# Transposes in groups inside two matrix products, and a reordered attention softmax, in a two-block transformer kernel

## Chip, cores and metric

One core of one Trainium2 chip. The metric is the device time of one execution in microseconds (us); a kernel's time is the median of its runs.

## Reference

Two transformer blocks on one sequence of 256 tokens, width 2048, float32. The change touches two steps of the first block, the attention over a memory of 256 tokens and the feed-forward step behind it:

```python
def memory_cross_attention(hn, mn, wq, wk, wv, wo):
    q = (hn @ wq).reshape(b, s, XA_HEADS, XA_HEAD_DIM)      # 4 heads of 128
    ...
    scores = jnp.einsum('bshd,bmhd->bhsm', q, k) * (XA_HEAD_DIM ** -0.5)
    probs = jax.nn.softmax(scores, axis=-1)
    o = jnp.einsum('bhsm,bmhd->bshd', probs, v).reshape(b, s, XA_WIDTH)
    return o @ wo

h = h + memory_cross_attention(rmsnorm(h, xa_norm_w), rmsnorm(mem, mem_norm_w), wq, wk, wv, wo)
u = rmsnorm(h, ffn_norm_w)
h = h + jnp.square(jax.nn.relu(u @ w1)) @ w2                 # w1: 2048 x 8192
```

Ahead of these stand the mixers and the product with `w_out`, behind them the second block with its experts.

## The kernel before

The products with weights are split into three: a weight is cast to a rounded half `wh` (ACT, line 289) and a remainder `wl` (DVE, line 290), the activation likewise into `uh` and `ul`, and PE sums `wh*uh + wh*ul + wl*uh`. Weights arrive in pieces of 1 MB (`raw`, three buffers), each holding four of the 16 chunks of 128 rows; `wsplit` casts two chunks at a time into `wh` and `wl`, of which there are three buffers each, so six chunks are cast at most ahead of PE. A cast of chunks 12 and 13 takes the buffer of chunks 6 and 7 and waits until PE has done with these. `gemm_T` takes 12 products of 256 columns per chunk, 192 in all, into one PSUM accumulator `acc` (two buffers).

The activation has to be transposed for it. `to_T` does this by chunks: two transposes on PE (line 254) into a PSUM tile `mx`, then ACT writes `uh` (line 367) and DVE writes `ul` (line 368), which needs `uh`. In `xattn` and in `ffn` all 16 chunks are asked for ahead of the product, then `rstd` takes the row norms: eight squares with sums on ACT (line 340) and a chain of some thirteen tiny operations on DVE (lines 355 to 273). The softmax needs them as its scale, lines 982 and 984; the feed-forward step needs them only when `w2`'s products are added.

In `xattn` the queries of all four heads are copied out of PSUM by one ACT instruction (line 987). Then, for each pair of heads, PE takes four score products, DVE the maximum (line 1000) and its scaled negative (line 1001), ACT the exponentials with their sums (line 1004), DVE the reciprocal and the scaling (lines 1006 and 1008), PE transposes the probabilities, DVE copies them (line 1017), and PE multiplies by the values.

All along DVE also works on something else: products of a modulation matrix for the second block (`macc`, line 830), fed by 512 KB loads.

The order on each engine isn't that of the source: a scheduler in the compiler sets it, and each engine then takes its own queue strictly in that order, stopping at an instruction whose input isn't there. The stretch in question is 773 to 873 us of the span.

Of the kernel before, what the change touches and what calls it, by code (L numbers as in the profile page):

```python
# [182 lines left out]
class Prog:  # L183
# [110 lines left out]

    def gemm_To(self, srcs, uh, ul, outs, widths):
        ncol = sum(widths)
        kg = srcs[0].shape[1]
        nk = kg * len(srcs)
        offs = [sum(widths[:j]) for j in range(len(widths))]
        for g, src in enumerate(srcs):  # L300
            for kc, h, l in self.wsplit(src, ncol):
                k = kg * g + kc
                for m, wd in enumerate(widths):
                    sl = slice(offs[m], offs[m] + wd)
                    for i, (a, b) in enumerate(((h, uh), (h, ul), (l, uh))):
                        self.mm(outs[m], a[:, sl], b[:, k, :], start=(k == 0 and i == 0 and m % 2 == 0),
                                stop=(k == nk - 1 and i == 2))

    def gemm_T(self, srcs, uh, ul):
        acc = self.acc()  # L310
        self.gemm_To(srcs, uh, ul, [acc[:, m * 256:m * 256 + 256] for m in range(4)], (128,) * 4)
        return acc
# [660 lines left out]
    def xattn(self):  # L973
        nc = self.nc
        r16 = lambda a: a.rearrange("p b (k t) -> p (b k) t", t=256)
        with ExitStack() as ctx:
            P = ctx.enter_context(self.tc.tile_pool(name="xa", bufs=2))
            uh, ul = r16(self.b16(F32R)), r16(self.b16(F32R))
            self.to_T([self.h[:, 0], self.h[:, 1]], lambda c: self.p("xa_w", c), uh, ul)
            rs = self.rstd(self.h)  # L980
# [3 lines left out]
            nc.vector.tensor_scalar(nsc, sc, -1.0, None, ALU.mult)  # L984
            acc = self.gemm_T([self.ins["wq"][g] for g in range(4)], uh, ul)
            qT = P.tile([128, 4, 256], F32, tag="qT", name="qT", bufs=1)
            nc.scalar.copy(qT, acc.rearrange("p (h t) -> p h t", h=4))
            xh = P.tile([128, 4, 256], F32R, tag="xh", name="xh", bufs=1)
            xl = P.tile([128, 4, 256], F32R, tag="xl", name="xl", bufs=1)
            S = lambda tag, n: self.smp.tile([128, n], F32, tag=tag, name=tag, bufs=2)  # L990
            for hp in range(2):
                ps = self.acc()
                for j in range(2):
                    h = hp * 2 + j
                    for tb in range(2):
                        o = j * 512 + tb * 256
                        self.mm(ps[:, o:o + 256], qT[:, h, tb * 128:tb * 128 + 128], self.kT[:, h], start=(tb == 0))
                mxv, nb, sm, ri = S("xmx", 4), S("xnb", 4), S("xsm", 4), S("xri", 4)
                v2 = lambda a: a.rearrange("p (j b) -> p j b", j=2)
# [26 lines left out]
    def ffn(self, extra):  # L1026
        nc = self.nc
        r16 = lambda a: a.rearrange("p b (k t) -> p (b k) t", t=256)
        with ExitStack() as ctx:
            P = ctx.enter_context(self.tc.tile_pool(name="ffn", bufs=2))  # L1030
            uh, ul = r16(self.b16(F32R)), r16(self.b16(F32R))
            self.to_T([self.h[:, 0], self.h[:, 1]], lambda c: self.p("ffn_w", c), uh, ul)
            rs = self.rstd(self.h)
            r2 = self.smp.tile([128, 2], F32, tag="r2", name="r2")
            nc.vector.tensor_tensor(r2, rs, rs, ALU.mult)

            def first(g):
                xh = P.tile([128, 8, 256], F32R, tag="fh", name="fh")
                xl = P.tile([128, 8, 256], F32R, tag="fl", name="fl")
                for j in range(2):  # L1040
                    acc = self.gemm_T([self.ins["w1"][g * 2 + j, k] for k in range(4)], uh, ul)
                    for b in range(2):
# [17 lines left out]
            self.final_init()  # L1060
            cur = first(0)
            for g in range(8):
                nxt = first(g + 1) if g < 7 else None
# [583 lines left out]
    def rows_hilo(self, P):  # L1647
# [4 lines left out]
        self.tc.keep_in_program_order(nc.vector.tensor_copy(rs2, self.rs))  # L1652
        self.busy(8)
        for q in range(4):
# [5 lines left out]

    def busy(self, n):
        ps = self.acc()
        for _ in range(n):
# [196 lines left out]
```

## Time and profile before

| | |
|---|---|
| median of 3 runs | 2301.49 us (2300.86, 2301.49, 2308.08) |
| the profiled execution | 2297.94 us, its span 2296.0 us |
| mean granted TensorE clock | 0.985 |
| PE busy (matmul) | 2165.3 us, 94% |
| DVE, ACT busy | 1502.9 us (65%), 892.8 us (39%) |
| DMA | 575.18 MB, mean 251 GB/s |

PE is TensorE's matmuls, PEld its weight loads, DVE VectorE, ACT ScalarE, SP the queue that issues the loads. Times are from the start of the span. "Idle before" an instruction is the time in which its engine stood, and `<-` names what released it.

### The profile page before, as it was taken

To read this page: it belongs to the slowest core of one execution; us is meant where nothing else is said; L and a number is where in the kernel's file an instruction comes from. 1 tells how busy PE (TensorE), PEld (TensorE's weight loads), DVE (VectorE), ACT (ScalarE), POOL (GpSimd) and SP (SyncE) were. 2 spreads that over 40 slices of the span, in tenths; PEclk is the share of its full clock that TensorE was granted. 3 is DMA by queue.
4 is the path that set the end of the run, shared out by engine and by line. 5 is a ranking of instruction groups with operands and counts; after the bars stand their busy time and mean duration, and the time that the engine had idled before them with its cause. 6 is when DMAs were issued, how large, how long until landed. Compare 5 with 4: busy or idle time off the path is not lost.

```text
span 2296.0 us, 40946 instructions
## 1 busy us (share of the span) xinstructions
PE 2165.3 (94%) x16688; PEld 1681.5 (73%) x16688; DVE 1502.9 (65%) x2561; ACT 892.8 (39%) x1445; POOL 61.4 (3%) x166
## 2 busy tenths in 40 slices
PE   6999999999999989999999999999999789888877
PEld 6888888888787779998998989988987442233222
DVE  6778887867768887778787787767657732222223
ACT  5444443444643444444444434446555211011000
POOL 1010000010100000000000000000000000000000
PEclk9999999999999999999999999999999999999899
DMA  7425443232278767887787787754445898999997
GB/s 255 146 96 184 157 165 134 95 114 93 86 284 310 282 251 260 289 304 268 263 313 257 258 314 259 268 183 156 167 164 195 332 379 367 393 395 421 420 421 319
DMA packets 101622, 575.18 MB, mean 251 GB/s; under 512 B 11548, under 2 KB 12700, under 8 KB 45880
## 3 DMA queue, kind: packets, MB, share of 16 engines
q1 hardware_dynamic: 101432, 572.55, 66.6%
q8 instruction: 132, 2.16, 0.4%
q14 instruction: 58, 0.48, 0.1%
HBM read 570.40 MB, written 2.10 MB: 249 GB/s over the span
## 4 chain that ended last, share of the span: by engine, by line
PE 75%; DMA 11%; DVE 9%; ACT 2%; issue 2%; SPq 0%; DVEq 0%; ACTq 0%
PE acc L250 43%; PE mx L250 30%; DMA mw<-wgu 4%; DMA mraw<-wmod 3%; DMA mw<-wd 2%; PE mx L254 2%; DVE wl L290 2%; DVE macc L830 1%; DMA row<-wmod 1%; DMA raw<-wd 1%; DMA b<-wgu 1%; ACT wh L289 0%; DMA raw<-wout 0%; DVE pr L1445 0%; DVE ey L1610 0%
## 5 line engine op out<-in xcount | busy, mean ns | idle before, releaser
L289 ACT CAST wh<-raw 128x1024 fp32r<-128x1024 f32 (+1 forms) x496 | 516.5, 1044 | 708.5 <-PE acc L250 521.9
L290 DVE TENSOR_TENSOR wl<-raw,wh 128x1024 fp32r<-128x1024 f32 (+1 forms) x496 | 599.0, 1213 | 191.6 <-ACT wh L289 189.2
L250 PE MATMUL acc<-b,wh 128*128 128x256 f32 x2560 | 467.4, 284 | 1.0 <-ACT b L367 1.0
L250 PE MATMUL mx<-b,wh 128*128 128x256 f32 (+1 forms) x2016 | 407.5, 292 | 0.7 <-ACT wh L289 0.7
L250 PEld LDWEIGHTS acc<-b,wh 128*128 128x128 f32 x2560 | 396.6, 189 | 3.2 <-ACT b L367 1.7
L250 PE MATMUL acc<-b,wl 128*128 128x256 f32 x1280 | 362.4, 283 | 0.6 <-DVE wl L290 0.6
L250 PEld LDWEIGHTS mx<-b,wh 128*128 128x128 f32 (+1 forms) x2016 | 314.9, 187 | 11.2 <-issue 3.3
L250 PE MATMUL mx<-b,wl 128*128 128x256 f32 (+1 forms) x1008 | 294.1, 292 | 0.8 <-DVE wl L290 0.8
L250 PEld LDWEIGHTS acc<-b,wl 128*128 128x128 f32 x1280 | 242.7, 190 | 1.7 <-DVE wl L290 1.4
L830 DVE SCALAR_TENSOR_TENSOR macc<-mraw,silc,macc 128x1024 f32<-128x1024 f32 x160 | 204.8, 1280 | 58.9 <-DMA mraw<-wmod 58.1
L250 PE MATMUL acc<-wh,fh 128*128 128x512 f32 x512 | 199.8, 390 | 0.0
L250 PE MATMUL acc<-wl,fh 128*128 128x512 f32 x512 | 199.3, 389 | 0.0
L250 PE MATMUL acc<-wh,fl 128*128 128x512 f32 x512 | 199.2, 389 | 0.0
L250 PEld LDWEIGHTS mx<-b,wl 128*128 128x128 f32 (+1 forms) x1008 | 188.2, 187 | 4.8 <-DVE wl L290 1.1
L250 PE MATMUL mx<-mw,xs 128*32 128x512 f32 (+1 forms) x512 | 122.8, 651 | 23.6 <-DMA mw<-wgu 21.7
L250 PE MATMUL acc<-wh,b 128*128 128x512 f32 x384 | 124.4, 402 | 1.0 <-ACT row L971 1.0
L250 PEld LDWEIGHTS acc<-wl,fh 128*128 128x128 f32 x512 | 96.1, 188 | 19.9
L250 PEld LDWEIGHTS acc<-wh,fl 128*128 128x128 f32 x512 | 96.1, 188 | 20.0
L250 PEld LDWEIGHTS acc<-wh,fh 128*128 128x128 f32 x512 | 96.1, 188 | 19.7
L250 PE MATMUL mx<-raw,xs 128*32 128x512 f32 (+1 forms) x328 | 98.1, 644 | 10.4 <-DMA raw<-wgu 10.4
L1580 DVE SCALAR_TENSOR_TENSOR eth<-eth,mx 128x256 f32<-128x256 f32 x9 | 3.8, 420 | 145.5 <-ACT eth L1579 145.5
L250 PEld LDWEIGHTS mx<-mw,xs 128*32 128x32 f32 (+1 forms) x512 | 26.8, 119 | 89.0 <-issue 44.2
(481 smaller groups left out, 2822.1 us busy)
## 6 DMA issues: line engine op xcount, KB each, us to landing
raw<-w SPq DMA_DIRECT2D x128, 1024.0 KB, 6.2
mraw<-wmod SPq DMA_DIRECT2D x160, 512.0 KB, 5.0
raw<-win SPq DMA_DIRECT2D x76, 1024.0 KB, 4.8
mw<-wgu SPq DMA_DIRECT2D x62, 1024.0 KB, 13.8
raw<-wgu SPq DMA_DIRECT2D x40, 1024.0 KB, 15.0
mw<-wd SPq DMA_DIRECT2D x28, 1024.0 KB, 15.1
raw<-wout SPq DMA_DIRECT2D x24, 1024.0 KB, 5.0
b<-wgu SPq DMA_DIRECT2D x23, 1024.0 KB, 10.9
```

The costliest lines, as they stand in the source:

```text
L250: return self.nc.tensor.matmul(out, lhsT=lhsT, rhs=rhs, start=start, stop=stop, skip_group_check=True)
L254: return self.nc.tensor.transpose(out, in_, self.ident[:k, :k])
L289: nc.scalar.copy(h[:, :n], rs)
L290: nc.vector.tensor_tensor(l[:, :n], rs, h[:, :n], ALU.subtract)
L830: nc.vector.scalar_tensor_tensor(a, b, self.silc[:, k:k + 1], a, ALU.mult, ALU.add)
L1580: nc.vector.scalar_tensor_tensor(th[:n], th[:n], 1.0, ps[:n, 0:256], ALU.add, ALU.mult)
```

## The change

The transposes are no longer asked for ahead of the product but inside it, four chunks before each weight piece, in `xattn` and in the first of `ffn`'s products. The norms (`rstd`) come after the product in the source, in `ffn` after the first two. The queries are copied out head by head, ACT and DVE in turn. The scores of all four heads are taken first, then seven products that nobody reads (`busy(7)`: a constant by a constant), then the softmax of both pairs.

```diff
@@ gemm_To
         for g, src in enumerate(srcs):
+            if before:
+                before(range(kg * g, kg * g + kg))
             for kc, h, l in self.wsplit(src, ncol):
...
@@ xattn
-            self.to_T([self.h[:, 0], self.h[:, 1]], lambda c: self.p("xa_w", c), uh, ul)
+            part = lambda ks: self.to_T([self.h[:, 0], self.h[:, 1]], lambda c: self.p("xa_w", c), uh, ul, ks)
+            acc = self.gemm_T([self.ins["wq"][g] for g in range(4)], uh, ul, part)
             rs = self.rstd(self.h)
...
-            acc = self.gemm_T([self.ins["wq"][g] for g in range(4)], uh, ul)
             qT = P.tile([128, 4, 256], F32, tag="qT", name="qT", bufs=1)
-            nc.scalar.copy(qT, acc.rearrange("p (h t) -> p h t", h=4))
+            for j in range(4):
+                (nc.vector.tensor_copy if j % 2 else nc.scalar.copy)(qT[:, j], acc[:, j * 256:j * 256 + 256])
...
+            scores = []
             for hp in range(2):
                 ps = self.acc()
...
                         self.mm(ps[:, o:o + 256], qT[:, h, tb * 128:tb * 128 + 128], self.kT[:, h], start=(tb == 0))
+                scores.append(ps)
+            self.busy(7, self.mx("lg"))
+            for hp, ps in enumerate(scores):
                 mxv, nb, sm, ri = S("xmx", 4), S("xnb", 4), S("xsm", 4), S("xri", 4)
@@ ffn
-            self.to_T([self.h[:, 0], self.h[:, 1]], lambda c: self.p("ffn_w", c), uh, ul)
-            rs = self.rstd(self.h)
-            r2 = self.smp.tile([128, 2], F32, tag="r2", name="r2")
-            nc.vector.tensor_tensor(r2, rs, rs, ALU.mult)
+            part = lambda ks: self.to_T([self.h[:, 0], self.h[:, 1]], lambda c: self.p("ffn_w", c), uh, ul, ks)
...
-                    acc = self.gemm_T([self.ins["w1"][g * 2 + j, k] for k in range(4)], uh, ul)
+                    acc = self.gemm_T([self.ins["w1"][g * 2 + j, k] for k in range(4)], uh, ul, None if g or j else part)
...
             cur = first(0)
+            rs = self.rstd(self.h)
+            r2 = self.smp.tile([128, 2], F32, tag="r2", name="r2")
+            nc.vector.tensor_tensor(r2, rs, rs, ALU.mult)
@@ busy
-    def busy(self, n):
-        ps = self.acc()
+    def busy(self, n, ps):
         for _ in range(n):
             self.tc.keep_in_program_order(self.mm(ps[:, 0:256], self.ones, self.c("run")))
```

What the scheduler makes of it is seen in three places. Lines of the changed kernel stand three to eight higher than those of before (370 for 367, 371 for 368, 343 for 340, 833 for 830, 1008 for 1000, 1012 for 1004). First, ACT from the second weight piece of `wq` to the exponentials; `wh<-raw` are casts of weights, `b_10231` is `uh`, `mx,ss` the squares, `qT` the queries. Before:

```order
L367 ACTIVATE b_10231<-mx,prm 128x256 x2
L289 CAST wh<-raw 128x1024
L367 ACTIVATE b_10231<-mx,prm 128x256 x11
L340 ACTIVATE mx,ss<-h 128x512
L367 ACTIVATE b_10231<-mx,prm 128x256
L340 ACTIVATE mx,ss<-h 128x512 x7
L289 CAST wh<-raw 128x1024 x7
L987 COPY qT<-acc 128x1024
L1004 ACTIVATE pr,xsm<-acc,xnb,xsc 128x256 x8
```

and in the changed kernel:

```order
L289 CAST wh<-raw 128x1024 x3
L370 ACTIVATE b_10231<-mx,prm 128x256 x4
L289 CAST wh<-raw 128x1024 x2
L370 ACTIVATE b_10231<-mx,prm 128x256 x3
L343 ACTIVATE mx,ss<-h 128x512
L370 ACTIVATE b_10231<-mx,prm 128x256
L343 ACTIVATE mx,ss<-h 128x512 x7
L289 CAST wh<-raw 128x1024
L991 COPY qT<-acc 128x256
L289 CAST wh<-raw 128x1024
L991 COPY qT<-acc 128x256
L1012 ACTIVATE pr,xsm<-acc,xnb,xsc 128x256 x8
```

The evacuations of chunks 8 to 15 and the eight squares, ahead of the last seven casts before, now stand among them, four chunks behind a cast each time, and the squares only two casts ahead of the exponentials.

Second, DVE from the last casts ahead of the scores to the first scaling of probabilities; `rs_`, `xsc` and `xnsc` are the chain of the norms, `xmx` the maxima, `xnb` what the exponentials wait for. Before:

```order
L290 TENSOR_TENSOR wl<-raw,wh 128x1024
L830 SCALAR_TENSOR_TENSOR macc<-mraw,silc,macc 128x1024
L290 TENSOR_TENSOR wl<-raw,wh 128x1024
L830 SCALAR_TENSOR_TENSOR macc<-mraw,silc,macc 128x1024
L1000 TENSOR_REDUCE xmx<-acc 128x4
L1001 TENSOR_TENSOR xnb<-xmx,xnsc 128x4
L1000 TENSOR_REDUCE xmx<-acc 128x4
L1001 TENSOR_TENSOR xnb<-xmx,xnsc 128x4
L830 SCALAR_TENSOR_TENSOR macc<-mraw,silc,macc 128x1024
L1006 RECIPROCAL xri<-xsm 128x4
L1008 TENSOR_SCALAR pr<-pr,xri 128x256 x4
```

and in the changed kernel, from the first maximum on:

```order
L1008 TENSOR_REDUCE xmx<-acc 128x4
L271 SCALAR_TENSOR_TENSOR rs_b<-rs_a,v_10565 128x2
L833 SCALAR_TENSOR_TENSOR macc<-mraw,silc,macc 128x1024
L273 SCALAR_TENSOR_TENSOR rs_y<-rs_b,rs_y 128x2
L1008 TENSOR_REDUCE xmx<-acc 128x4
L269 TENSOR_TENSOR rs_a<-rs_y 128x2
L833 SCALAR_TENSOR_TENSOR macc<-mraw,silc,macc 128x1024
L271 SCALAR_TENSOR_TENSOR rs_b<-rs_a,v_10565 128x2
L273 SCALAR_TENSOR_TENSOR rs_y<-rs_b,rs_y 128x2
L986 TENSOR_SCALAR xsc<-rs_y 128x2
L988 TENSOR_SCALAR xnsc<-xsc 128x2
L1009 TENSOR_TENSOR xnb<-xmx,xnsc 128x4 x2
```

Before, the norms were there when the first maximum was taken, and `xnb` followed it; now both maxima, two `macc` steps and the last seven tiny steps of the norms stand ahead of `xnb`. Ahead of this piece stand the norms' first steps with two casts (`wl`) and two of the four copies of the queries. The four copies of `qT` wait for each other in the order of the heads, ACT, DVE, ACT, DVE, since all write one tile, and the scores of the second pair take the buffer that the copies read.

Third, DVE where `ffn` begins; `b_10840` and `b_10851` are `ul`. Before:

```order
L290 TENSOR_TENSOR wl<-raw,wh 128x1024
L941 TENSOR_TENSOR h<-acc,h 128x512 x2
L368 SCALAR_TENSOR_TENSOR b_10840<-mx,prm,b_10839 128x256 x12
L290 TENSOR_TENSOR wl<-raw,wh 128x1024
L368 SCALAR_TENSOR_TENSOR b_10840<-mx,prm,b_10839 128x256 x2
```

and in the changed kernel:

```order
L290 TENSOR_TENSOR wl<-raw,wh 128x1024 x2
L944 TENSOR_TENSOR h<-acc,h 128x512 x2
L290 TENSOR_TENSOR wl<-raw,wh 128x1024
L371 SCALAR_TENSOR_TENSOR b_10851<-mx,prm,b_10850 128x256 x5
L290 TENSOR_TENSOR wl<-raw,wh 128x1024 x2
L371 SCALAR_TENSOR_TENSOR b_10851<-mx,prm,b_10850 128x256 x4
L290 TENSOR_TENSOR wl<-raw,wh 128x1024 x2
L371 SCALAR_TENSOR_TENSOR b_10851<-mx,prm,b_10850 128x256 x4
```

A cast has moved ahead of the first chunk's `ul`, and each further group of four chunks stands behind two casts. On PE the products go with it: in both places the transposes stand in groups of six or eight in front of the products of their weight piece, where before most were spread by twos between the products of chunks 2 to 6.

## Rows read from the trace of the kernel before

**Rows 1.** Page, part 4: chain that ended last, shares of the span by engine.

```profile
PE 75%; DMA 11%; DVE 9%; ACT 2%; issue 2%; SPq 0%; DVEq 0%; ACTq 0%
```

**Rows 2.** Stretches; per engine: busy us (instructions), granted clock, DMA share, GB/s.

```profile
773.25:783.50 10.25, 5.87 (x29) 5.43 (x28) 9.14 (x12) 2.68 (x5) 0.00 (x0) 0.67 0.90 336
783.50:787.70 4.20, 3.28 (x25) 2.36 (x23) 2.11 (x5) 2.84 (x5) 0.95 (x1) 1.00 0.54 207
787.70:810.20 22.50, 22.50 (x183) 21.82 (x182) 20.22 (x39) 14.62 (x31) 0.00 (x0) 1.00 0.72 272
810.20:819.04 8.84, 3.72 (x17) 2.96 (x17) 7.95 (x11) 5.24 (x15) 0.00 (x0) 1.00 0.73 254
...
821.00:828.00 7.00, 6.38 (x16) 4.98 (x17) 5.00 (x11) 0.75 (x2) 0.00 (x0) 0.51 0.47 155
```

**Rows 3.** Timeline before product wq: DVE, then PE; start, us, instruction, [idle <-releaser].

```profile
776.28 1.28 DVE L830 SCALAR_TENSOR_TENSOR macc<-mraw,silc,macc 128x1024 f32<-128x1024 f32 x1 [1.00 <-DMA mraw<-wmod]
...
778.62 0.69 PE L254 MATMUL mx<-cst,h 128*128 128x128 f32 x2 [4.04 <-DVE b L368]
```

**Rows 4.** Groups by shape, 770 to 880 us: xcount | busy, mean ns | idle.

```profile
L290 DVE TENSOR_TENSOR wl<-raw,wh 128x1024 fp32r<-128x1024 f32 x26 | 31.6, 1219 | 7.7 <-ACT wh L289 7.6
L830 DVE SCALAR_TENSOR_TENSOR macc<-mraw,silc,macc 128x1024 f32<-128x1024 f32 x23 | 29.4, 1278 | 1.7 <-DMA mraw<-wmod 1.5
L289 ACT CAST wh<-raw 128x1024 fp32r<-128x1024 f32 x26 | 26.9, 1051 | 44.9 <-PE acc L250 33.9 <-DMA raw<-wq 9.1 <-DVE rs_y L273 1.9
...
L367 ACT ACTIVATE b<-mx,prm 128x256 fp32r<-128x256 f32 x32 | 14.1, 473 | 1.9 <-PE mx L254 1.3
L368 DVE SCALAR_TENSOR_TENSOR b<-mx,prm,b 128x256 fp32r<-128x256 f32 x32 | 13.8, 478 | 2.6 <-ACT b L367 2.3
...
L1000 DVE TENSOR_REDUCE xmx<-acc 128x4 f32<-128x1024 f32 x2 | 2.4, 1224 | 0.8 <-PE acc L250 0.8
```

**Rows 5.** Timeline of PE in the attention.

```profile
812.13 3.72 PE L250 MATMUL acc<-row,qT 128*128 128x256 f32 x16 [1.93 <-ACT qT L987]
819.04 1.33 PE L254 MATMUL mx<-cst,pr 128*128 128x128 f32 x8 [3.19 <-DVE pr L1008]
821.62 3.78 PE L250 MATMUL mx<-pT,row 128*128 128x256 f32 x8 [1.25 <-DVE pT L1017]
...
830.29 1.89 PE L250 MATMUL mx<-pT,row 128*128 128x256 f32 x8
```

**Rows 6.** Timeline of ACT: copy, exponentials, later two squares.

```profile
811.07 1.01 ACT L987 COPY qT<-acc 128x1024 f32<-128x1024 f32 x1
815.68 0.56 ACT L1004 ACTIVATE pr<-acc,xnb,xsc 128x256 f32<-128x256 f32 x1 [3.60 <-DVE xnb L1001]
...
817.86 0.57 ACT L1004 ACTIVATE pr<-acc,xnb,xsc 128x256 f32<-128x256 f32 x1
...
859.36 0.60 ACT L340 ACTIVATE mx<-h 128x512 f32<-128x512 f32 x1
...
859.97 0.60 ACT L340 ACTIVATE mx<-h 128x512 f32<-128x512 f32 x1
```

**Rows 7.** Timeline of DVE in the softmax.

```profile
817.23 1.28 DVE L830 SCALAR_TENSOR_TENSOR macc<-mraw,silc,macc 128x1024 f32<-128x1024 f32 x1
818.42 0.17 DVE L1006 RECIPROCAL xri<-xsm 128x4 f32<-128x4 f32 x1
818.63 1.14 DVE L1008 TENSOR_SCALAR pr<-pr,xri 128x256 f32<-128x256 f32 x4
```

**Rows 8.** Timeline of PE where product w1 starts.

```profile
850.86 1.04 PE L254 MATMUL mx<-cst,h 128*128 128x128 f32 x8
852.53 0.39 PE L250 MATMUL acc<-b,wh 128*128 128x256 f32 x1 [0.64 <-ACT b L367]
853.33 0.44 PE L254 MATMUL mx<-cst,h 128*128 128x128 f32 x2 [0.41 <-DVE b L368]
```

More of the change, by code (lines that the diff above doesn't have):

```diff
@@ L292, in wsplit, with gemm_To @@
                 yield j + kc, h[:, kc * ncol:kc * ncol + ncol], l[:, kc * ncol:kc * ncol + ncol]
-    def gemm_To(self, srcs, uh, ul, outs, widths):
+    def gemm_To(self, srcs, uh, ul, outs, widths, before=None):
         ncol = sum(widths)
@@ L307, in gemm_To, with gemm_T @@
                                 stop=(k == nk - 1 and i == 2))
-    def gemm_T(self, srcs, uh, ul):
+    def gemm_T(self, srcs, uh, ul, before=None):
         acc = self.acc()
-        self.gemm_To(srcs, uh, ul, [acc[:, m * 256:m * 256 + 256] for m in range(4)], (128,) * 4)
+        self.gemm_To(srcs, uh, ul, [acc[:, m * 256:m * 256 + 256] for m in range(4)], (128,) * 4, before)
         return acc
@@ L1652, in rows_hilo @@
         self.tc.keep_in_program_order(nc.vector.tensor_copy(rs2, self.rs))
-        self.busy(8)
+        self.busy(8, self.acc())
         for q in range(4):
```

## The prediction

> **What bounds the kernel now.** I began with the chain of waits on the page, because it says whose time the end hangs on: PE carries 75% of it, DVE 9% and DMA 11% [rows 1]. Before the last stage with its experts nothing else is near, so a microsecond that PE stands or works slowly in the stretch touched is a microsecond of the result, and one that another engine saves counts only if PE was waiting for it. The table of stretches then shows how PE fares there, and the reader is to see three kinds in it [rows 2]. From 787.70 to 810.20 the product with wq runs without a hole: 183 instructions in 22.50 us, 0.123 us each, with eleven chunks' transposes among them. Here nothing is to be won. Ahead of that, 773.25 to 787.70, PE is busy 9.15 us of 14.45. And from 810.20 to 819.04, the softmax, it is busy for 3.72 of 8.84 us, and afterwards works at 0.51 of the full clock, that is at the lower of its two levels.
>
> The timelines tell why. The hole before the product is one wait of 4.04 us for the first `ul`, which on DVE stands behind a `macc` step that waited for its load [rows 3]. In the attention PE waits 1.93 us for the copy of the queries, 3.19 us for the first scaled probabilities, 1.25 us for their transposed copy [rows 5]. The low level costs about 3.2 us, half of the 6.38 us that PE works from 821 to 828 [rows 2]: eight records of value products take 3.78 us there, and eight more of them 1.89 us once the clock is full again [rows 5].
>
> **The groups in the product with wq.** The first wait of 4.04 us stays: on DVE the rows up to the first two `ul` are the same in both orders, the late load included. The stretch 783.50 to 787.70 keeps its modulation transposes and reductions in the same place; fewer transposes stand there, so it may gain up to 1.8 us, what remains of its 4.20 us when 18 transposes of 0.13 us (eight in 1.04 [rows 8]) are all that PE does. I take 0, since the wait for DVE behind the same two reductions is still there.
>
> New are the hand-overs at chunks 8 and 12. The third buffer of casts decides: the cast of chunks 12 and 13 must wait until PE is done with chunk 7 (of the 44.9 us that ACT stood before casts, 33.9 were such waits [rows 4]), and the evacuation of chunk 8 is now queued behind that cast. From the end of chunk 7 on, ACT casts 1.05 us and evacuates 0.47, so `uh` is there at 1.52 us, when PE has been through its eight transposes at 1.04: idle 0.48. DVE gets the cast at 1.05, takes 1.22 for `wl` and 0.48 for `ul`, 2.75 in all; PE was ready at 1.64: idle 1.11 [rows 4]. At chunk 12 six transposes take 0.78, `uh` comes at 1.52 again (idle 0.74), and the last two transposes wait for a PSUM tile that DVE frees at 2.00, PE being there at 1.64 (0.36). Together 2.7 us; about 0.2 us of short waits for `wl` before go. **+2.5 us.** Below, it can be 0 if the casts come early; above, 3.5.
>
> **The softmax.** In mean durations; times from here on count from the end of the product unless they say otherwise. ACT has, from the end of chunk 11 on, a cast (1.05), four evacuations (some 1.7 us) and eight squares that follow each other by 0.61 us [rows 6]: done at 7.65. PE has the waits and transposes just counted (2.26) and 47 products of 0.123: it ends at 8.04, so the squares are done 0.4 us before. A cast of wo comes next (to 0.65), then the first copy: nearest row, an evacuation of the same 128x256, 0.47. So the scores begin at 1.1 us instead of 1.93: won 0.8. But the second copy is DVE's, and there the first four steps of the norms and a `wl` that waits for that cast stand first: it ends at 2.55; the third at 3.0 on ACT; another `wl` (1.22) and two tiny steps at 0.2 each bring the fourth to 4.65. Only then is the buffer free for the second pair's scores: 4.65 to 6.5, by 3.72 us for all eight [rows 5]. The seven idle products, at 0.465 us each by the same row, keep PE until 9.8. Meanwhile DVE does what the order shows ahead of `xnb`: maximum 1.22, `macc` 1.28, maximum 1.22, `macc` 1.28 [rows 4], and nine steps of 0.2: 6.8 us, from 4.65 to 11.45. The exponentials of the first pair take 2.18 us [rows 6], reciprocal and first scaling 0.5 [rows 7]: the probabilities' transposes begin at 14.1, before at 8.84. The long instructions overlap their successors a little (a `macc` step of 1.28 at 817.23, the next at 818.42 [rows 7]), 0.1 us for some eight of them: 13.3. **+4.5 us.** Bounds: 0 if the norms are early, so that the 0.8 won at the scores pays for the rest, +6.5 if a `macc` step waits for its load.
>
> So the idle products fill 3.3 us of a hole that grows by more. From 9.8 to 13.3 PE stands 3.5 us, and before it stood 3.19 us ahead of the fall to the lower level. I take the low stretch as unchanged: 0, between -3.2 (it doesn't fall) and +1 (it falls a little earlier). What follows, from the transposes of the first pair to the last product with wo, has the same DVE order up to the second pair and no hole on PE before: 0, with 0.5 either way.
>
> **The groups in ffn.** Before, PE waits 0.64 and 0.41 us there and then runs on [rows 8]. Now one `wl` more stands ahead of the first `ul`: 1.2 us, of which PE's other work takes 0.4: +0.8. The group of chunks 5 to 8 has chunk 4's twelve products (1.5 us) as cover for the 2.75 us of cast, `wl`, `ul`; with the transposes that leaves 0.2. The next has no cover, and both casts stand first on DVE: 0.74 + 1.11 = 1.85. The last, among which PE mixes products of the next column block: 0.9. **+3.7 us**, between +1 and +5. The norms, moved behind, are wanted only when w2's products are added, at least another 192 products of 0.123 us later: nothing.
>
> **Sum.** 2.5 + 4.5 + 0 + 3.7 = +10.7 us. The profiled execution took 2297.94 us, its span 2296.0; with the change 2308.6. The median of the three runs, 2301.49, is 3.55 above the profiled one, so for a median I forecast **2312 us**, slower by 0.46%. 0.3%, 6.9 us, is about what a measurement of this kernel can tell from no change.
>
> **Rivals.** *The clock holds.* If the second pair's copies and the norms come early, the 3.5 us on the idle side shrink under the 3.19 that were too long before; the full level then saves 3.2 us, and the softmax costs nothing more (0.8 won at the scores, the rest hidden by the idle products). What is left are the hand-overs: 2.5 + 3.7 - 3.2 = +3.0, 2304.5 us, not slower by the bound. It decides at `xnb`: it must be ready by about 7 us after the product instead of 11.4. For it speaks that the seven products run exactly where PE stood; against it the queue on DVE. The Trainium skill, "TensorE: Matmul & The Clock Gate", section "Why this matters for your kernels", asks to leave no long idle gap between bursts of products, as the clock else goes back to its low level; by that rule the seven products are worth the 3.2 us. The trace of before agrees on the fall (0.51 after 821), and on nothing yet about what prevents it. Chance 0.19; with the hand-overs at their lower bounds (0 and 1), 1.8 us won at 783.50 and the 0.8 at the scores kept it would come near -5 us, and the rest to the bound is within what such sums miss; I leave 0.05 of it for that.
>
> *Only the hand-overs.* The norms' chain finishes ahead of the maxima, since DVE is idle more than its order suggests: the softmax then costs 0 and the clock falls as before: 2.5 + 0 + 3.7 = +6.2, 2307.7 us. Against it: the squares end only about when the product does. Chance 0.16.
>
> *Late loads.* The `macc` steps ahead of `xnb` wait for their 512 KB, as one did for 1.00 us at 776.28 [rows 3]; two such waits and the hole behind grow the softmax by 2 to 4 us more: 2315 us. Chance 0.08.
>
> **How the numbers follow.** The forecast case has 0.57, from +7 to +13 us, 0.04 of it under the bound. Slower by over 0.3%: 0.53 + 0.02 of the second rival + 0.08 of the third = 0.63. Within 0.3%: 0.04 + 0.14 of the first + 0.14 of the second = 0.32. Faster by over 0.3%: 0.05. The range from 2300 to 2317 leaves out the lowest part of the first rival and the highest of the third.
>
> **What would show it.** In the new profile: two waits of PE for `uh` and `ul` of 0.4 to 1.2 us at chunk 8 of wq, and at chunk 8 of w1; scores that begin about 1 us after the product, but the second pair's over 4 us after; `xnb` more than 9 us after; a hole of 3 to 4 us between the idle products and the transposes, and the lower clock level behind it. It is wrong if the transposes of the probabilities start within 10 us of the product's end, if the clock stays at its full level until the products with wo, or if PE has no waits inside the two products.

## The result, and the profile after

The changed kernel took 2314.14 us, median of 11 runs (2310.69 to 2321.75), against 2301.12 us for the kernel before, likewise 11 runs (2295.17 to 2315.4), taken beside them. The ratio is 1.0055 with a 95% interval of 1.004 to 1.007: slower by some 13 us. The forecast was 2312. The profiled execution has a span of 2309.5 us, 13.5 more than the one of before.

PE's part of the chain that ended last has gone from 75% [rows 1] to 71%; DVE and DMA have gained (page of the changed kernel, part 4):

```profile
PE 71%; DMA 13%; DVE 10%; ACT 3%; issue 2%; SPq 0%; DVEq 0%; ACTq 0%
```

The table of stretches, columns as in [rows 2]: from the first transpose for wq to the product's end, from there to the first product with wo, the work at the lower clock (it begins in that stretch and reaches 0.8 us beyond it), and the part of the first w1 product in which the clock falls to that level once more.

```profile
775.50:814.58 39.08, 32.52 (x233) 30.19 (x231) 31.27 (x43) 19.49 (x40) 0.95 (x1) 0.91 0.79 286
814.58:832.62 18.04, 12.44 (x48) 9.60 (x47) 15.85 (x35) 6.64 (x21) 0.00 (x0) 0.83 0.63 210
826.91:833.40 6.49, 5.94 (x18) 4.75 (x19) 5.24 (x11) 2.00 (x8) 0.00 (x0) 0.51 0.54 184
...
877.70:881.10 3.40, 3.40 (x18) 3.40 (x18) 0.48 (x1) 2.45 (x9) 0.00 (x0) 0.50 0.00 0
```

What PE waited for in these stretches, in its timeline (start us, duration, instruction, in brackets the idle time and what ended it):

```profile
798.76 0.38 PE L250 MATMUL acc<-b,wh 128*128 128x256 f32 x1 [0.57 <-ACT b L370]
800.05 0.39 PE L250 MATMUL acc<-b,wh 128*128 128x256 f32 x1 [0.90 <-DVE b L371]
...
807.33 0.39 PE L250 MATMUL acc<-b,wh 128*128 128x256 f32 x1 [0.74 <-ACT b L370]
808.52 0.44 PE L254 MATMUL mx<-cst,h 128*128 128x128 f32 x2 [0.80 <-DVE b L371]
...
815.10 1.13 PE L250 MATMUL acc<-row,qT 128*128 128x256 f32 x4 [0.52 <-ACT qT L991]
816.42 1.13 PE L250 MATMUL acc<-row,qT 128*128 128x256 f32 x4 [0.18 <-DVE qT L991]
818.02 1.99 PE L250 MATMUL acc<-row,qT 128*128 128x256 f32 x8 [0.48 <-DVE qT L991]
819.86 3.19 PE L250 MATMUL mx<-cst 128*128 128x256 f32 x14
826.91 1.94 PE L254 MATMUL mx<-cst,pr 128*128 128x128 f32 x8 [3.87 <-DVE pr L1016]
829.40 3.78 PE L250 MATMUL mx<-pT,row 128*128 128x256 f32 x8 [0.55 <-DVE pT L1025]
...
859.27 0.38 PE L250 MATMUL acc<-b,wh 128*128 128x256 f32 x1 [0.64 <-ACT b L370]
860.67 0.44 PE L254 MATMUL mx<-cst,h 128*128 128x128 f32 x2 [1.02 <-DVE b L371]
...
869.41 0.39 PE L250 MATMUL acc<-b,wh 128*128 128x256 f32 x1 [0.23 <-DVE b L371]
...
875.26 0.39 PE L250 MATMUL acc<-b,wh 128*128 128x256 f32 x1 [0.73 <-ACT b L370]
876.54 0.44 PE L254 MATMUL mx<-cst,h 128*128 128x128 f32 x2 [0.90 <-DVE b L371]
```

The four new waits at chunks 8 and 12 of wq are together 3.01 us. The scores start at once, but the transposes of the probabilities stand 3.87 us behind the idle products, and the low clock is where it was. DVE's timeline over the softmax tells why:

```profile
817.95 1.22 DVE L1008 TENSOR_REDUCE xmx<-acc 128x4 f32<-128x1024 f32 x1
819.09 0.15 DVE L271 SCALAR_TENSOR_TENSOR rs_b<-rs_a,v 128x2 f32<-128x2 f32 x1
819.16 1.28 DVE L833 SCALAR_TENSOR_TENSOR macc<-mraw,silc,macc 128x1024 f32<-128x1024 f32 x1
...
820.42 1.22 DVE L1008 TENSOR_REDUCE xmx<-acc 128x4 f32<-128x1024 f32 x1
...
821.62 1.28 DVE L833 SCALAR_TENSOR_TENSOR macc<-mraw,silc,macc 128x1024 f32<-128x1024 f32 x1
...
823.61 0.24 DVE L1009 TENSOR_TENSOR xnb<-xmx,xnsc 128x4 f32<-128x4 f32 x2
```

Norm steps, maxima and modulation sums (`macc`) alternate, and `xnb` for both pairs starts 9.0 us after the product's end at 814.58 and is done at 9.3.

Stage by stage, the profiled spans differ thus (from starts and ends in the two timelines of PE, and for w1 the start of the Relu that evacuates a product on ACT):

| stage | before | after | difference |
|---|---|---|---|
| span's start to the first wq transpose (not touched) | 773.25 | 775.50 | +2.25 |
| to the end of the wq product | 36.95 | 39.08 | +2.1 |
| to the first wo product | 14.64 | 18.04 | +3.4 |
| to the first transpose for w1 | 26.02 | 24.98 | -1.0 |
| to the evacuation of the fourth w1 product | 100.4 | 104.6 | +4.2 |
| to the last evacuation of w1 products | 544.0 | 548.0 | +4.0 |
| to the end | 800.7 | 799.2 | -1.5 |

The four middle stages, which the forecast was about, lose 8.7 us; the other 4.8 us of this pair of profiles lie outside them.

### The profile page after: what moved, and what is told of

It reads as the page before. It is cut to its first block, busy times and chain, and to the rows that moved or that the text cites. A ratio compares the mean times of both kernels' runs of the same rounds, so it can differ in the third digit from the quotient of the medians.

```text
span 2309.5 us, 40976 instructions
## 1 busy us (share of the span) xinstructions
PE 2175.7 (94%) x16702; PEld 1691.3 (73%) x16702; DVE 1505.1 (65%) x2563; ACT 892.4 (39%) x1446; POOL 61.6 (3%) x166
## 4 chain that ended last, share of the span: by engine, by line
PE 71%; DMA 13%; DVE 10%; ACT 3%; issue 2%; SPq 0%; DVEq 0%; ACTq 0%
PE acc L250 38%; PE mx L250 31%; DMA mraw<-wmod 4%; DMA mw<-wgu 4%; DVE wl L290 2%; DMA mw<-wd 2%; PE mx L254 2%; DVE macc L833 2%; DMA b<-wgu 2%; DMA raw<-wd 1%; ACT wh L289 1%; DMA raw<-win_s 0%; DMA raw<-wout 0%; DVE pr L1453 0%; DMA row<-wmod 0%
## 6 DMA issues: line engine op xcount, KB each, us to landing
b<-wgu SPq DMA_DIRECT2D x23, 1024.0 KB, 11.4
```

## Experiments

The same stages in the profiles of all kernels; "ratio" is against the kernel before in the same comparison, with its 95% interval.

| kernel | wq product | to first wo | first wq transpose to 4th w1 evacuation | 4th to last | ratio |
|---|---|---|---|---|---|
| before | 36.9 | 14.6 | 178.0 | 544.0 | 1 |
| changed | 39.1 | 18.0 | 186.7 | 548.0 | 1.0055 (1.004 to 1.007) |
| e1 no idle products | 38.7 | 21.7 | 190.4 | 545.3 | 1.0058 (1.0035 to 1.008) |
| e2 norms inside | 37.8 | 13.9 | 183.2 | 547.9 | 1.0025 (1.0007 to 1.0044) |
| e3 groups asked ahead | 35.6 | 18.5 | 178.3 | 557.9 | 1.0058 (1.0039 to 1.0077) |
| e4 both | 38.2 | 16.8 | 178.5 | 556.0 | 1.0012 (0.999 to 1.0035) |
| e5 softmax only | 36.9 | 17.9 | 179.8 | 546.0 | 0.9991 (0.9969 to 1.0013) |
| e6 ffn as before | 40.2 | 20.2 | 185.7 | 545.0 | 1.004 (1.0012 to 1.0067) |
| e7 asked ahead, ffn as before | 36.6 | 22.2 | 187.9 | 545.8 | 1.0036 (1.0011 to 1.0061) |
| e8 as e7, norms inside | 35.9 | 14.4 | 176.1 | 548.2 | 0.9994 (0.9974 to 1.0015) |
| e9 as e6, sums held | 42.8 | 12.8 | 181.5 | 548.0 | 1.001 (0.9986 to 1.0035) |
| e10 as e8, sums held | 37.5 | 12.5 | 176.3 | 546.9 | 0.9988 (0.9967 to 1.0008) |
| e11 as e5, sums held | 35.3 | 12.5 | 174.5 | 548.7 | 0.9984 (0.9959 to 1.0009) |
| e12 before, sums held | 36.3 | 14.8 | 178.2 | 546.0 | 0.9986 (0.9963 to 1.0008) |

Two things limit what a row says. The stages are those of one execution, the ratio is that of all: e4's profile took 2314.05 us where its median is 2307.82, e3's 2309.89 where it is 2313.73. And the first column holds PE's wait for the first `ul`, which stands behind a sum and its load: it was 1.80 us in e2, 2.69 with the change, 2.70 in e3, 4.72 in e9 and 5.73 in e4, whatever the edit.

**e1, the idle products.**

```
-            self.busy(7, self.mx("lg"))
```

> The changed kernel without its idle products. Theory (the idle products only fill a hole that the late norms and maxima open): the first probability transposes still come about 12.3 us after the wq product ends (12.33 with the idle products), and the time is that of the changed kernel or up to 3 us more, if PE then stays longer at the lower clock: +13 to +16 us against the kernel before, 1.0055 to 1.007. Rival (the idle products themselves hold up the softmax): their 3.19 us come off, the transposes start at about 9 us, +10 us, 1.004.

The ratio is that of the change. In this execution the transposes came even later, 16.0 us after the product, but not for want of idle products: the scores of the second head waited 2.57 us for a copy on DVE, which stood behind a sum that had waited 3.35 us for its load (timeline of DVE, then of PE):

```profile
812.52 1.28 DVE L833 SCALAR_TENSOR_TENSOR macc<-mraw,silc,macc 128x1024 f32<-128x1024 f32 x1 [3.35 <-DMA mraw<-wmod]
```

```profile
816.09 1.13 PE L250 MATMUL acc<-row,qT 128*128 128x256 f32 x4 [2.57 <-DVE qT L991]
...
827.76 1.94 PE L254 MATMUL mx<-cst,pr 128*128 128x128 f32 x8 [6.53 <-DVE pr L1015]
```

Taking the products away made nothing earlier. The rival's 1.004 lies within the interval, so the time alone doesn't exclude it; what speaks against it is the profile of the change, where PE had been through the idle products and stood another 3.87 us for DVE. In e1 PE then worked at the lower clock from 824.3 to 834.5 us, longer than with the products; whether for want of them or because the copy was late, this run can't separate.

**e2, the norms.**

```
+            def part(ks):
+                self.to_T([self.h[:, 0], self.h[:, 1]], lambda c: self.p("xa_w", c), uh, ul, ks)
+                if ks[0] == 4:
+                    rs.append(self.rstd(self.h))
...
-            rs = self.rstd(self.h)
```

> The changed kernel, but the norms of the hidden state (eight squares on ACT and the short steps on DVE) are asked for behind the second group's transposes, inside the wq product, not behind the product. Theory (the softmax is late because norms, maxima and the scaled bounds queue up on DVE behind the product): the scaled bounds of the second pair come at 4 to 6 us after the product's end in place of 9.0, the first probability transposes within 9 us in place of 12.3; the eight squares in front of weight casts cost the product up to 1.5 us; the sum is -2 to -3.5 us against the changed kernel, so +9.5 to +11 us against the kernel before, 1.004 to 1.005. Rival (the two pairs' maxima and the modulation sums on DVE are enough to fill that time): transposes stay past 11 us, and the time stays at +13 us, 1.0055, or rises by the squares.

The first wo product came at 13.9 us, less than before the change, with 0.003 less on the ratio, some 7 us (1.0025 against 1.0055; the intervals just touch). That is more than the 2 to 3.5 us of the theory, and more than the 3.5 us that the stages of this profile gained. But `xnb` split in two: the first pair's at 5.4 us after the product's end (813.01), the second's at 11.2, since a sum that waited for its load stood ahead of the second maximum, and another sum and the first pair's scaling behind it (timeline of DVE):

```profile
818.26 0.16 DVE L1013 TENSOR_TENSOR xnb<-xmx,xnsc 128x4 f32<-128x4 f32 x1
819.42 1.28 DVE L833 SCALAR_TENSOR_TENSOR macc<-mraw,silc,macc 128x1024 f32<-128x1024 f32 x1 [0.99 <-DMA mraw<-wmod]
...
823.01 1.14 DVE L1020 TENSOR_SCALAR pr<-pr,xri 128x256 f32<-128x256 f32 x4
824.07 0.15 DVE L1013 TENSOR_TENSOR xnb<-xmx,xnsc 128x4 f32<-128x4 f32 x1
```

The transposes therefore began at 10.4 us, not within 9, and the gain came where the first pair no longer waits for the second. The rival, transposes past 11 us and no gain, falls too. The squares in front of the casts cost the product nothing that the profile shows.

**e3 and e4, the hand-overs.** Each group's transposes are asked for ahead of the second half of the group before, here in both products; e4 adds e2's edit.

```
-            if before:
-                before(range(kg * g, kg * g + kg))
+            if before and g == 0:
+                before(range(kg))
             for kc, h, l in self.wsplit(src, ncol):
                 k = kg * g + kc
+                if before and kc == kg // 2 and g + 1 < len(srcs):
+                    before(range(kg * g + kg, kg * g + 2 * kg))
```

> The changed kernel, but each group of four transposed chunks is asked for half a group earlier, ahead of the products with the weight piece before it, in both products. Theory (the waits at the hand-overs are evacuations queued behind weight casts): the waits for uh and ul at chunks 8 and 12 (0.57, 0.90, 0.74, 0.80 us in wq; 0.23, 0.73, 0.90 us in w1) fall to 0.3 us together or less, the wq product with its transposes takes 36.5 us or less in place of 39.08, the low-clock stretch in the first w1 product goes; the softmax stays at 12 us; together -4.5 to -6 us against the changed kernel: +7 to +8.5 us against the kernel before, 1.003 to 1.0037. Rival (casts are pushed back instead, and PE waits for weights where it waited for chunks): the product keeps its 39 us, +13 us, 1.0055.

> Norms inside the product and the groups asked for half a group ahead, together. Theory (these two are all that the change costs, and they don't share their time): the two gains add up, -7 to -9.5 us against the changed kernel, so +3.5 to +6 us against the kernel before, 1.0015 to 1.0025; what is left over is the later waits of the w2 products on DVE. Rival (the change can gain once its two queues are mended, because the first wq product starts after a quarter of the transposes): the kernel before or better, 0.998 to 1.0005. Rival (the squares meet the evacuations, and one of the two gains is lost): +7 us or more, 1.003.

In the profile of e3 the waits at the hand-overs are gone from both products, the wq product takes 35.6 us, and at the fourth w1 evacuation 178.3 us have passed, as before the change (178.0), 8.4 us less than with it. The first wait is the same as with the change (2.70 and 2.69 us), so this comparison is clean. The time over all runs is none the better. From the fourth evacuation to the last evacuation it lost 9.9 us against the changed kernel; e4 lost 8.0 there. The waits of PE in that stretch (total us, times, longest; e3):

```profile
PE acc L250 <- DVE wl L290: 5.8, 5, 1.8
PE mx L254 <- DVE macc L835: 2.1, 1, 2.1
```

and DVE's timeline at one of them:

```profile
998.54 1.28 DVE L835 SCALAR_TENSOR_TENSOR macc<-mraw,silc,macc 128x1024 f32<-128x1024 f32 x1 [0.44 <-DMA mraw<-wmod]
999.74 0.75 DVE L948 SCALAR_TENSOR_TENSOR h<-acc,r,h 128x512 f32<-128x512 f32 x1
1002.49 1.28 DVE L835 SCALAR_TENSOR_TENSOR macc<-mraw,silc,macc 128x1024 f32<-128x1024 f32 x1 [2.00 <-DMA mraw<-wmod]
1003.70 2.35 DVE L290 TENSOR_TENSOR wl<-raw,wh 128x1024 fp32r<-128x1024 f32 x2
```

The scheduler had let the sums of the first modulation halves run during the first two w1 products; with the groups' evacuations in those places it put them off, and they now stand between residual additions of the w2 products, each waiting for its load, with two weight differences behind it that PE wants. Waits of PE for DVE from 900 to 1590 us are 7.9 us in e3 and 2.3 in the changed kernel, and behind two of them PE worked at half the clock for 3.4 us each (0.50 from 1006.1 and from 1077.8). An edit in one stage was paid for in another, more than 100 us later. e4 is at 1.0012, a little better than its first theory's 1.0015 to 1.0025, but its interval takes in e2 alone and part of the rival that the mended change gains (0.998 to 1.0005); that the two gains add up isn't shown. Of e3 the theory was right in its stages and wrong in the time (1.0058, not 1.003 to 1.0037), and its rival, that the product keeps its 39 us, falls.

**e5, e6, e7 and e8** separate these. e5 undoes both groupings and keeps the softmax; e6 undoes the one in ffn alone, by

```
-            part = lambda ks: self.to_T([self.h[:, 0], self.h[:, 1]], lambda c: self.p("ffn_w", c), uh, ul, ks)
+            self.to_T([self.h[:, 0], self.h[:, 1]], lambda c: self.p("ffn_w", c), uh, ul)
...
-                    acc = self.gemm_T([self.ins["w1"][g * 2 + j, k] for k in range(4)], uh, ul, None if g or j else part)
+                    acc = self.gemm_T([self.ins["w1"][g * 2 + j, k] for k in range(4)], uh, ul)
```

and the norm moved back; e7 is e6 with e3's edit for wq alone, e8 is e7 with e2's.

> The change without its groups: all sixteen transposes ahead of both products and the ffn's norm ahead of its product, as before; queries copied by heads, all scores first, idle products, norms asked for behind the product, as in the change. In the built order ACT takes the squares between the casts of the wq product here, since all evacuations are issued early, and VectorE's order in the w1 and w2 products is that of the kernel before. Theory (what the softmax lost is that the groups push the squares to the product's end, and the order by scores alone is no loss): scores 0.5 to 1.3 us and the second pair's bounds 4 to 7 us after the product, first wo product 13 to 14.7 us after the product's end against 14.64 before and 18.03 with the change; 0 to -2 us against the kernel before, 0.999 to 1.000. Rival (the softmax by scores first is itself dearer): first wo product at 17 us or later, +3 us or more, 1.0013 or above.

> The changed kernel with the groups of the first w1 product undone (its sixteen transposes and the ffn's norm ahead of the product, as before); groups in wq and the softmax as changed. Theory (the w1 groups cost their hand-overs, a stretch at the lower clock, and a shift of VectorE's modulation sums in the w1 and w2 products): first evacuation of w1 30 to 31 us after the first ffn transpose, as before, in place of 36.2; the later part of the ffn, from its fourth evacuated w1 product to its last, back to 544 us in place of 548; -5 to -8 us against the changed kernel, so +5 to +8 us against the kernel before, 1.002 to 1.0035. Rival (that the later 4 us are chance, not a matter of the order): -4.2 us alone, +8.8 us, 1.0038.

> Groups asked for half a group ahead as in the run that did so in both products, but in wq alone; the w1 product's transposes and norm ahead of it, as before; softmax as changed. The first 178 us from the first wq transpose were no longer there than before in that run, and 12.6 us were lost later, in the w1 and w2 products of the second and third steps, where VectorE's modulation sums had moved among the residual additions. Theory (the moved sums are that loss, since each waits for its load in front of a weight difference): with the order of the kernel before in the ffn those 12.6 us are gone, 544 to 546 us from the fourth evacuated w1 product to the last; 0 to +2 us against the kernel before, 1.000 to 1.001. Rival (loads come late there by chance or by the earlier end of the softmax, whatever the order): 550 us or more, +6 us or more.

> The same with the norms asked for inside the wq product, behind the second group. Theory (hand-overs, late norms and displaced sums are all that the change lost, and the rest of it gains): the wq product with its transposes 35.5 to 37 us, first wo product 14 us after the product, the ffn as before: -1 to -3 us against the kernel before, 0.9987 to 0.9996. Rival (nothing is left to gain, the first weight waits and the loads of the modulation sums set the start whatever is done): 1.000 to 1.0015. Rival (squares on ACT in front of casts): product 38 us, as in the run with both, +1 to +2 us.

*The displaced sums* are confirmed in the profiles: with the order of before in the ffn, e7 takes 545.8 us for the later part where e3 took 557.9. *The w1 groups:* e6 has 31.3 us from the first transpose to the first evacuation (30.7 before, 36.2 with the change), and no fall of the clock there. But the 4.0 us that the changed kernel lost in the later part are not its order: e1, with that same order, took 545.3, and the kernels with an even order range from 544.0 to 548.7. My reading of them, on record for e6, falls; they are within what executions differ by, as the rival had it, and e6's ratio, 1.004, lies nearest to the rival's 1.0038 (its interval holds the theory's 1.002 to 1.0035 too). In the time over all runs e7 missed its theory (1.000 to 1.001), since its softmax was late, while e8 met its own in both stages and the time; but e8's interval also holds its rival, that nothing is left to gain (1.000 to 1.0015).

*The softmax* went against e5's expectation in the profile, 17.9 us to the first wo product in place of 13 to 14.7, and e6 and e7 took 20.2 and 22.2. The timelines of DVE in e5 (first row) and e6 (its product ended at 815.99) show the cause:

```profile
819.32 1.28 DVE L833 SCALAR_TENSOR_TENSOR macc<-mraw,silc,macc 128x1024 f32<-128x1024 f32 x1 [3.80 <-DMA mraw<-wmod]
```

```profile
815.59 1.28 DVE L833 SCALAR_TENSOR_TENSOR macc<-mraw,silc,macc 128x1024 f32<-128x1024 f32 x1 [2.23 <-DMA mraw<-wmod]
...
818.68 0.42 DVE L991 COPY qT<-acc 128x256 f32<-128x256 f32 x1
...
827.15 0.24 DVE L1009 TENSOR_TENSOR xnb<-xmx,xnsc 128x4 f32<-128x4 f32 x2
```

A modulation sum waits 3.80 us in e5 and 2.23 us in e6 for its 512 KB, and in e6 norms, weight difference, query copy and maxima queue behind it. In the time over all runs e5 is level with the kernel before and apart from the change, as its theory had it. That the softmax by scores first is itself dearer is not borne out by that time, but its 1.0013 is the interval's end, and this profile has the 17 us or more that it named; e11 below, the same softmax without the sums, takes 12.5. e7 and e8 differ by the place of the norms alone, and by 7.8 us in the stage, of which late loads of e7's execution are a part that these runs don't separate.

**e9 to e12, the sums held back.** On VectorE the ffn's sums may not be issued before the softmax's last instruction, and the first of their halves is asked for ahead of the first w1 product:

```
+            self.late = self.last_on("DVE")
             for q in range(4):
...
+            with self.tc.issue_after(self.late):
+                extra.pop(0)()
             cur = first(0)
...
-                    extra.pop(0)()
+                    with self.tc.issue_after(self.late):
+                        extra.pop(0)()
```

> As the run with the w1 groups undone (wq by groups and the softmax as changed, the ffn's transposes and norm ahead), with the modulation sums of the ffn held back on VectorE until the softmax's last instruction, and the first of their halves asked for ahead of the first w1 product, not behind it. Theory (VectorE is late for the softmax because these sums, each waiting for its load, stand between the last weight differences, the query copies, the norm steps and the maxima): no sum between chunk 8 of wq and the last value product; the second query copy waits under 0.6 us (it waited 1.44 us there), the second pair's bounds come 5 to 7 us after the product in place of 11.4, the first wo product at 12 to 15 us in place of 20.2; -5 to -8 us against that run: +1 to +4 us against the kernel before, 1.0005 to 1.002. Rival (the norm steps and maxima alone fill that time): the first wo product past 17 us, +7 us or more, 1.003.

> The mended version (wq's groups asked for half a group ahead, norms inside the product, the ffn as before), with the same sums held back and the first half ahead of the first w1 product. Theory: wq product 35.5 to 37 us, first wo product 11 to 13 us after the product in place of 14.4 (14.64 before); with the sums' order even through the w1 and w2 products, 544 to 546 us for the later part of the ffn: -3 to -6 us against the kernel before, 0.9974 to 0.9987. Rival (held sums come back as waits in the first w1 product or the w2 products, where VectorE now has sixteen or more to catch up): 0 us or slower, 1.000 or above.

> Softmax of the change alone (all transposes ahead of both products, as before), with the sums held back in the same way. Theory: first wo product 11.5 to 13 us after the product (17.9 in the run without holding, 14.64 before), second pair's scores under 4 us (7.07), -1.5 to -4 us against the kernel before, 0.9983 to 0.9994. If it equals the run with asked-ahead groups within 0.001, the groups bring nothing even when they cost nothing; if it is slower than that one by 1.5 us or more, the early start of the product is worth that. Rival (held sums come back later): 1.000 or above.

> The kernel before with nothing but the sums held back and the first half asked for ahead of the first w1 product. It tells what of the gain of the two runs beside it is the holding alone. Theory (in the kernel before the sums cost the softmax less, because scores and maxima follow one another by pairs and the norms were ready): first wo product 13 to 14.6 us after the product, 0 to -2 us, 0.999 to 1.000. Rival (the holding is the whole gain, the order by scores is none): as fast as the softmax run beside it, within 0.0005.

In e9 the norms are still behind the product, and yet the second pair's `xnb` is at 7.0 us after its end (817.54), in place of 11.4 in e6, and the first wo product at 12.8, in place of 20.2. In the order on DVE the norm steps now also run through ahead of the first maximum. The time is 1.001 against e6's 1.004, with intervals that overlap. DVE's timeline of e9:

```profile
822.93 0.16 DVE L1009 TENSOR_TENSOR xnb<-xmx,xnsc 128x4 f32<-128x4 f32 x1
823.12 1.22 DVE L1008 TENSOR_REDUCE xmx<-acc 128x4 f32<-128x1024 f32 x1
824.38 0.17 DVE L1009 TENSOR_TENSOR xnb<-xmx,xnsc 128x4 f32<-128x4 f32 x1
```

And the clock held. The stretch from the product's end to the first wo product has a granted clock of 0.76 in e6 (first row) and 1.00 in e9 (second):

```profile
815.99:836.16 20.17, 14.01 (x47) 10.53 (x47) 17.36 (x40) 6.71 (x21) 0.00 (x0) 0.76 0.55 189
```

```profile
817.54:830.35 12.81, 10.97 (x54) 8.70 (x55) 10.12 (x29) 6.83 (x21) 0.00 (x0) 1.00 0.24 83
```

So did it in e10 and e11. It held in e2 and e8 too, where sums were left in and the second pair's `xnb` was late (11.2 and 9.6), but the first pair's came at 5.4 and 5.8 and PE stood only 1.25 and 1.63 us behind the idle products, against 3.87 with the change; e2's stretch:

```profile
813.01:826.93 13.92, 10.53 (x47) 7.79 (x47) 12.39 (x21) 6.47 (x20) 0.00 (x0) 1.00 0.69 235
```

In e11's timeline of PE the idle products end where the transposes begin, without a wait:

```profile
811.43 1.13 PE L250 MATMUL acc<-row,qT 128*128 128x256 f32 x4 [1.29 <-ACT qT L991]
812.75 2.86 PE L250 MATMUL acc<-row,qT 128*128 128x256 f32 x12 [0.19 <-DVE qT L991]
815.44 3.19 PE L250 MATMUL mx<-cst 128*128 128x256 f32 x14
818.46 1.26 PE L254 MATMUL mx<-cst,pr 128*128 128x128 f32 x8
```

Of the time, little of it arrives. The held sums come back in the first w1 product, where one weight difference is late by 1.55 us (e11, and the same in e9 and e10):

```profile
859.38 0.39 PE L250 MATMUL acc<-b,wl 128*128 128x256 f32 x1 [1.55 <-DVE wl L290]
```

e10, e11 and e12 lie at 0.9984 to 0.9988 and can't be told from each other, nor from the kernel before (the upper ends are 1.0008 and 1.0009). That e12, which keeps the old softmax, does as well says that neither the scores first nor the groups have a gain of their own that these runs can show. No version is shown to beat the kernel before. Whether idle products are worth something once nothing stands between them and the transposes wasn't tried.

## Why the prediction was right

The forecast of 2312 us was 2.1 us low, and that is closer than its sum deserves. The medians differ by 13 us, the stages that the sum of 10.7 was about by 8.7; some 4 us are not accounted for by what was touched, and by the time alone the rival of late loads (2315) is nearer. What was right is the mechanism: hand-overs in both products and a late softmax with the lower clock behind it. The terms, against the profile of the changed kernel:

- **Groups in the wq product, +2.5:** +2.1. The waits at the two hand-overs are 0.57 and 0.90 (0.48 and 1.11 were worked out), 0.74 and 0.80 (0.74 and 0.36; a sum that waited for its load held the `ul` that the last two transposes wait for), together 3.0. The first wait was 2.69 us in place of 4.04, since the load ahead of it came sooner in this execution, other short waits shrank by 0.4, and PE's busy time in the stage rose by 0.9, from 31.65 by the same view, which was not in the sum. So 3.0 - 1.35 - 0.4 + 0.9 met a forecast of 2.5: the waits were right, the last three cancel by chance. e3 shows the cause: asked for half a group earlier, the waits vanish and the product takes 35.6 us.
- **Softmax, +4.5:** +3.4 here. Scores came at 0.5 us (1.1), the second pair's at 3.4 (4.65, and over 4 was named as a sign), `xnb` was done at 9.3 (11.45), the transposes came at 12.3 (13.3). The steps on DVE were sized too dear. The start gave 0.6 us of it: the squares on ACT were done 0.9 us ahead of the product's end, not 0.4, and the first copy took 0.37 us, not 0.47. Up to the fourth copy another 0.6 us fell away, and from the first maximum to `xnb` DVE took 5.9 us in place of 6.8, since a norm step between two long instructions added some 0.07 us (819.09 to 819.16), not 0.2; the 0.8 us that the forecast took off at its end for overlap cover a part of this. In executions where a sum waited 2 us or more for its load, e1, e6 and e7, whose softmax has the same work on DVE, the first wo product came at 20 to 22 us: 2 to 4 us more than here. That is the rival of late loads, with the price it had. How often the changed kernel itself runs so isn't known from its one profile, but 0.08 looks too small.
- **Clock, 0:** the low level was there as long as before, but it now covered 0.8 us of the wo stage (832.62 to 833.40) where it had covered 3 (824.84 to 828 [rows 2]), and 1.0 us came back there. It fell a second time, in the w1 product (0.50 from 877.70 to 881.10, after waits of 0.73 and 0.90 us), which costs half of 3.40, 1.7 us, and was not forecast.
- **Groups in ffn, +3.7:** +4.2. The waits of PE there are 3.8 us against 1.05 before [rows 8], +2.75, and 1.7 come from the clock. By groups the waits were: at the start 0.64 and 1.02, 0.6 more than before (0.8 was worked out); for chunks 5 to 8, 0.23 (0.2); for the next, 0.73 and 0.90 (1.85); for the last, 0.3 (0.9). So the hand-overs were sized rightly but for the last one, and the right total was reached because the fall of the clock, which the sum lacked, made up for it.
- **What lay outside:** the stages further on, and the one ahead, differ by +4.0, -1.5 and +2.25. The first is within what the runs spread in that stage; of the other two no run shows a cause.

One reason was weighed wrongly. The queue on DVE was named as the cause of the late softmax, with the norms at its head, and the two sums as 2.6 us in it. With the sums held and the norms left behind the product in the source, the stage takes 12.8 us (e9). With the norms inside the product and the sums left in, it takes 13.9 and 14.4 us (e2, e8), but 16.8 in e4, where a sum waited 1.68 us for its load ahead of a query copy. So the sums make most of it, by their 1.28 us each between the norm steps and by their own waits for loads; the norms alone don't.

The rival that the clock holds did not come about in the change, but its condition, "ready by about 7 us after the product", was met in three runs, and in all three the clock held. In e9 to e11 `xnb` is done at 6.9 to 7.0 us, PE has no wait ahead of the transposes, and the granted clock is 1.00 to the first wo product. It need not hold for both pairs: in e2 and e8 the clock held with the first pair's `xnb` early and the second's at 11.2 and 9.6. The Trainium skill, "TensorE: Matmul & The Clock Gate", section "Why this matters for your kernels", asks for no long idle gap between bursts of products; these rows agree with it. The fall in the w1 product, behind waits of 0.73 and 0.90 us, isn't explained so. By e1, idle products in a hole that stays longer than they are change nothing that the time shows.

## What to carry to other kernels

An instruction that is moved takes its place in an in-order queue: ask for each group's input half a weight piece before it is needed, so that its evacuation stands ahead of a cast and not behind it. Background work that waits for loads on the engine that evacuates is the first thing to look for where a short dependent chain is late; and if a scheduler places it, look at its order in the stages after an edit as well, since an edit that wins 8 us in its own stage can lose 10 us there. Idle products in a hole that outlasts them brought nothing here that the time shows.

## What was not expected of the hardware

The same code ahead of the change took from 773.1 us (e1) to 784.2 us (e12) up to the first wq transpose. Stretches at the lower clock make part of it, and which there are differs by execution. The longest, in e12, lies where PE is busy 20.90 of 21.00 us; a pause of 1.20 us stands 1.6 us ahead of it:

```profile
606.41 0.38 PE L250 MATMUL mx<-ip,itt 32*32 32x32 f32 x22 [1.20 <-issue]
```

```profile
608.00:629.00 21.00, 20.90 (x160) 17.42 (x159) 7.78 (x18) 9.61 (x19) 1.72 (x6) 0.51 0.15 51
```

In the kernel before, whose instructions are the same there, with the same pause of 1.16 us at 602.82, the stage ran at the full clock:

```profile
560.00:640.00 80.00, 75.04 (x1013) 63.12 (x1011) 62.57 (x204) 47.40 (x110) 6.43 (x13) 1.00 0.33 119
```

So a busy PE was granted half the clock for 21 us in one execution and all of it in another, behind the same pause; what decides is open. A single profile of this kernel can't tell 5 us by its span. Stages from a common start tell more, but not that much either: the later part of the ffn took from 544.0 to 548.7 us in the kernels whose sums were not displaced.
